# Larger row blocks in fewer buffers: five blocks of 32 and 56 rows per partition in place of eight of 32

## Chip, cores and metric

One core of a Trainium2 chip runs the kernel. The metric is the device time of one execution in microseconds (us); lower is better. All ratios below use runs in the fast state, against runs of the kernel before on the same chip in the same session; a slow run (over 1.5% above the fastest of the same kernel) is named and left out. Runs 1 to 4, 5 to 8 and 9 to 11 had one chip and session each, in which the kernel before took 163.67, 163.64 and 163.60 us, so times may be compared across them to some tenths of a us. A ratio is the mean time of one kernel's fast runs over the mean of the other's fast runs of the same rounds, so it is not quite the ratio of the medians that are quoted.

## The reference

```python
x: (16, 2048, 256) float32          # 32768 rows of 256
W_adapted    = W + scale * (lora_A @ lora_B)                  # 256 x 256
W_norm       = np.sqrt(np.sum(W_adapted ** 2, axis=0, keepdims=True) + 1e-8)
W_final      = W_adapted / W_norm * m
y            = x.reshape(-1, 256) @ W_final                   # float32 out
```

Computing `W_final` is small. The bulk is to read 33.6 MB of x, multiply by one 256 x 256 matrix, and write 33.6 MB of y.

## The kernel before

x is cut into blocks; a block gives every partition `DJ` = 32 consecutive rows of 1 KB, so its load has one 32 KB descriptor per partition (a descriptor is one contiguous piece of a transfer; the trace records each as one packet, 128 for a load). A transfer has *landed* when the last of the 16 DMA engines has reported its completion. The result overwrites x in the same SBUF buffer and is stored from there. There are five such buffers.

```python
DJ = 32; NBLK = 8; XBUFS = 5
...
parts = [(b * CH, CH) for b in range(NBLK - 1)]                # seven whole blocks
parts += [(NCH - CH, CH // 2), (NCH - CH // 2, CH // 2)]       # the last: two halves
...
for n in range(len(parts)):                  # SyncE: all loads
    b = parts[n][0] // CH
    if b >= XBUFS and parts[n][0] % CH == 0:
        nc.sync.wait_ge(sem(f"store{b - XBUFS}"), 16)          # buffer free?
    load_x(n)
```

The compute is a pipeline over 32 *pairs*, a pair being 8 rows per partition (two groups of `J` = 4 rows). GpSimd rounds a pair to bf16, TensorE transposes it, VectorE copies the transposes to SBUF, TensorE multiplies, ScalarE copies the two halves of the product back into the x buffer and issues the store when a stored part is complete. TensorE's loop handles two pairs per turn:

```python
turned(0)
with nc.Fori(0, NPR // 2, 1, engines=[PE], head_slot={PE: 128}):
    turned(1)      # transposes of pair 2i+1: waits until it is rounded
    product(0)     # product of pair 2i
    product(1)     # product of pair 2i+1
    turned(0)      # transposes of pair 2i+2
```

So the product of an even pair stands *behind* the transposes of the odd pair after it. With blocks of 32 rows (4 pairs), every block begins at an even pair, and the two never belong to different blocks.

## Time and profile before

| | before |
|---|---|
| time, median | 163.63 us (163.5 to 163.79) |
| span of the profiled execution | 163.2 us (this execution took 164.71) |
| busy share PE, ACT, POOL, DVE | 65%, 39%, 38%, 29% |
| bytes moved, mean rate | 67.41 MB, 413 GB/s |

From the page of the kernel before, the span in 40 equal slices of 4.08 us; a digit is the busy share in tenths, 9 meaning 90% or more:

```profile
## 2 busy tenths in 40 slices
PE   1270599789789897898981998619988820892000
DMA  5998998998999999999999999999999999998991
GB/s 201 402 498 386 426 474 385 482 418 265 466 426 426 442 410 466 426 394 482 418 426 442 420 426 458 402 458 410 446 414 454 414 446 422 450 442 377 442 430 60
```

The DMA row is at 8 or 9 from the second slice to the last but one, while TensorE has idle slices at the end. The 265 GB/s of the tenth slice is the one dip of the middle. The queue part of the same page (queue, packets, megabytes, share of 16 engines' span) says the same in sums:

```profile
q1 hardware_dynamic: 1440, 33.82, 49.0%
q10 hardware_dynamic: 1474, 33.59, 47.8%
```

q1 carries the loads, q10 the stores; together they fill 96.8%. The kernel is bound by its DMA engines. Waits of compute engines are therefore harmless as long as transfers stay queued. The waits of the kernel before (engine, line, what it waited for, total us, times, longest):

```profile
ACT x_sb L219 <- PE y_ps L281: 75.8, 33, 13.2
POOL xb L165 <- DMA x_sb<-in_x_dram: 56.0, 6, 12.2
```

GpSimd waits 56 us for loads, ScalarE 75.8 us for products, and neither costs anything here. The chain that ended last ascribes to them only the end:

```profile
## 4 chain that ended last, share of the span: by engine, by line
ACT 1%; PE 1%; issue 0%
```

Last, how long a block's compute takes once its load has landed. This is the second half of the last block, from the timeline of the kernel before (start, duration, engine, line, operation, and in brackets the idle time before it and what ended it; L165 rounds, L219 copies the product, L128 issues the store):

```profile
137.23 3.73 POOL L165 CAST xb<-x_sb 128x2048 bf16<-128x2048 f32 x2 [11.14 <-DMA x_sb<-in_x_dram]
143.94 1.93 ACT L219 COPY x_sb<-y_ps 128x1024 f32<-128x1024 f32 x2 [11.19 <-PE y_ps L281]
148.20 0.34 ACTq L128 DMA_DIRECT2D out_dram<-x_sb  x1
```

16 rows need 11.0 us from the first rounding to the issue of the store.

### The profile page before, as it was taken

To read this page: it belongs to the slowest core of one execution; us is meant where nothing else is said; L and a number is where in the kernel's file an instruction comes from. 1 tells how busy PE (TensorE), PEld (TensorE's weight loads), DVE (VectorE), ACT (ScalarE), POOL (GpSimd) and SP (SyncE) were. 2 spreads that over 40 slices of the span, in tenths; PEclk is the share of its full clock that TensorE was granted. 3 is DMA by queue.
4 is the path that set the end of the run, shared out by engine and by line. 5 is a ranking of instruction groups with operands and counts; after the bars stand their busy time and mean duration, and the time that the engine had idled before them with its cause. 6 is when DMAs were issued, how large, how long until landed. Compare 5 with 4: busy or idle time off the path is not lost. (4 is left out here: it accounts for less than half of the span.)

```text
span 163.2 us, 1988 instructions
## 1 busy us (share of the span) xinstructions
PE 105.3 (65%) x786; PEld 85.2 (52%) x786; DVE 47.2 (29%) x44; ACT 63.8 (39%) x67; POOL 62.5 (38%) x39
## 2 busy tenths in 40 slices
PE   1270599789789897898981998619988820892000
PEld 0130577677577775776760867418676610771000
DVE  0429452350532514405230325005051400330000
ACT  3010027548366384473754053900738440062000
POOL 1006381753935738268004940069209003900000
PEclk9999999999999999999998589985899996599755
DMA  5998998998999999999999999999999999998991
GB/s 201 402 498 386 426 474 385 482 418 265 466 426 426 442 410 466 426 394 482 418 426 442 420 426 458 402 458 410 446 414 454 414 446 422 450 442 377 442 430 60
DMA packets 2915, 67.41 MB, mean 413 GB/s; under 512 B 465, under 2 KB 482, under 8 KB 610
## 3 DMA queue, kind: packets, MB, share of 16 engines
q1 hardware_dynamic: 1440, 33.82, 49.0%
q10 hardware_dynamic: 1474, 33.59, 47.8%
q14 instruction: 1, 0.01, 0.0%
HBM read 33.85 MB, written 33.55 MB: 413 GB/s over the span
## 5 line engine op out<-in xcount | busy, mean ns | idle before, releaser
L219 ACT COPY x_sb<-y_ps 128x1024 f32<-128x1024 f32 x64 | 61.9, 1014 | 75.8 <-PE y_ps L281 75.8
L165 POOL CAST xb<-x_sb 128x2048 bf16<-128x2048 f32 x32 | 60.0, 1902 | 79.3 <-DMA x_sb<-in_x_dram 56.0
L281 PE MATMUL y_ps<-w_final,xt 128*128 128x256 bf16 x512 | 64.6, 280 | 12.8 <-PEq L256 12.8
L202 DVE COPY xt<-xt_ps 128x1024 f32<-128x1024 f32 x32 | 38.2, 1221 | 88.1 <-PE xt_ps L267 88.0
L281 PEld LDWEIGHTS y_ps<-w_final,xt 128*128 128x128 bf16 x512 | 48.4, 100 | 28.2 <-issue 19.8
L267 PE MATMUL xt_ps<-identity,xb 128*128 128x128 f32 x264 | 39.1, 309 | 23.1 <-PEq L256 23.1
L267 PEld LDWEIGHTS xt_ps<-identity,xb 128*128 128x128 f32 x264 | 34.9, 161 | 25.8 <-issue 25.6
L198 DVE TENSOR_TENSOR w_final<-wam,rnorm 128x256 bf16<-128x256 f32 x2 | 4.0, 2028 | 0.0
L244 PE MATMUL y_ps<-sq,ones 128*128 128x256 f32 x4 | 2.1, 674 | 1.6 <-DVE sq L187 1.6
L233 PE MATMUL y_ps<-identity,a_nat 128*16 128x128 f32 x2 | 0.6, 397 | 3.6 <-DMA a_nat<-in_lora_A_dram 3.6
L212 ACT ACTIVATE norm<-y_ps,eps_col 128x256 f32<-128x256 f32 x1 | 0.5, 473 | 6.1 <-PE y_ps L244 6.1
L244 PEld LDWEIGHTS y_ps<-sq,ones 128*128 128x128 f32 x4 | 1.2, 323 | 2.3 <-DVE sq L187 2.1
L210 ACT ACT_TABLE_LOAD x1 | 1.3, 1283 | 2.4 <-issue 2.4
L233 PEld LDWEIGHTS y_ps<-identity,a_nat 128*16 128x16 f32 x2 | 0.1, 90 | 3.6 <-issue 3.6
L171 POOL MEMSET xb<- 128x2048 bf16 x1 | 1.8, 1805 | 0.3 <-PE xt_ps L267 0.3
L195 DVE RECIPROCAL rnorm<-norm 128x256 f32<-128x256 f32 x1 | 1.7, 1745 | 0.0
L237 PE MATMUL y_ps<-b_bf,aT 16*128 16x256 bf16 x2 | 0.6, 404 | 1.5 <-DVE aT L180 1.5
L189 DVE COPY m_all<-y_ps 128x256 f32<-128x256 f32 x1 | 0.4, 425 | 3.3 <-PE y_ps L249 3.3
L178 DVE CAST b_bf<-b_nat 16x256 bf16<-16x256 f32 x1 | 0.3, 281 | 3.8 <-DMA b_nat<-in_lora_B_dram 3.8
L249 PE MATMUL y_ps<-m_row,ones 1*128 1x256 f32 x2 | 1.2, 710 | 0.0
L237 PEld LDWEIGHTS y_ps<-b_bf,aT 16*128 16x128 bf16 x2 | 0.1, 106 | 1.9 <-DVE aT L180 1.9
L183 DVE SCALAR_TENSOR_TENSOR wa<-y_ps,w_nat 128x512 f32<-128x512 f32 x1 | 0.7, 692 | 0.8 <-PE y_ps L237 0.8
(13 smaller groups left out, 3.7 us busy)
## 6 DMA issues: line engine op xcount, KB each, us to landing
x_sb<-in_x_dram SPq DMA_DIRECT2D x7, 4096.0 KB, 27.1
out_dram<-x_sb ACTq DMA_DIRECT2D x7, 4096.0 KB, 37.2
x_sb<-in_x_dram SPq DMA_DIRECT2D x2, 2048.0 KB, 29.6
out_dram<-x_sb ACTq DMA_DIRECT2D x2, 2048.0 KB, 20.2
w_nat<-in_W_dram SPq DMA_DIRECT2D x1, 256.0 KB, 2.9
a_nat<-in_lora_A_dram ACTq DMA_DIRECT2D x1, 16.0 KB, 2.6
b_nat<-in_lora_B_dram ACTq DMA_DIRECT2D x1, 16.0 KB, 3.6
m_row<-in_m_dram ACTq DMA_DIRECT2D x1, 1.0 KB
```

The costliest lines, as they stand in the source:

```text
L165: nc.gpsimd.tensor_copy(out=xb_bufs[p % NXB][:], in_=x_bufs[b % XBUFS][:, 2 * c * J : 2 * (c + 1) * J, :],).then_inc(sem("rounded"), 1)
L171: nc.gpsimd.memset(xb_bufs[NPR % NXB][:], 0.0).then_inc(sem("rounded"), 1)
L183: nc.vector.scalar_tensor_tensor(out=wa[:], in0=ab_ps, scalar=float(scale), in1=w_nat[:], op0=ALU.mult, op1=ALU.add).then_inc(dv, 1)
L195: nc.vector.reciprocal(out=rnorm[:], in_=norm[:]).then_inc(dv, 1)
L198: i = nc.vector.tensor_mul(out=w_final[:, t], in0=wam[:, t], in1=rnorm[:])
L202: nc.vector.tensor_copy(out=xt_bufs[p % NXT][:].rearrange("p r t -> p (r t)").bitcast(FP32), in_=xt_ps[p % 2][:],).then_inc(sem("copied"), 1)
L210: nc.scalar.activation(out=warm[:], in_=eps_col[:], func=AF.Sqrt)
L219: nc.scalar.copy(out=x_bufs[b % XBUFS][:, c * J : (c + 1) * J, :], in_=y_ps[g % 2][:]).then_inc(sem("room"), 1)
L244: i = nc.tensor.matmul(n2_ps, ones[:], sq[:, t, :], start=(t == 0), stop=(t == KC - 1))
L249: nc.tensor.matmul(mb_ps, ones[0:1, :], m_row[:], start=True, stop=True).then_inc(pe, 1)
L267: i = nc.tensor.transpose(xt_ps[p % 2][:, j * P : (j + 1) * P], xb_bufs[p % NXB][:, j, :].bitcast(FP32), identity[:],)
L281: i = nc.tensor.matmul(y_ps[h][:, j, :], xt_bufs[p % NXT][:, r : r + P, t], w_final[:, t, :], start=(t == 0 and (j % (J // 2)) == 0), stop ...
```

## The change

The intent: fewer and longer descriptors (up to 56 KB in place of 32 KB) save a fixed cost on each. 168 KB of buffers per partition take the place of 160 KB, hence three buffers of 56 rows. The diff, cut to its core:

```diff
-    DJ = 32
-    BLK = DJ * P
-    NBLK = N // BLK
-    XBUFS = 5
+    BLOCKS = [32, 56, 56, 56, 56]
+    STORES = [[32], [56], [56], [56], [24, 16, 16]]
+    DJ = max(BLOCKS)
+    XBUFS = 3
 ...
-    parts = [(b * CH, CH) for b in range(NBLK - 1)]
-    parts += [(NCH - CH, CH // 2), (NCH - CH // 2, CH // 2)]
 ...
+    def load_x(b):                      # one load for each block, the last too
         nc.sync.dma_start(
-            out=in_sbuf(*parts[n]), in_=in_dram(x_flat, *parts[n])
-        ).then_inc(sem(f"load{n}"), 16)
+            out=x_bufs[b % XBUFS][:, 0 : BLOCKS[b], :], in_=in_dram(x_flat, b)
+        ).then_inc(sem(f"load{b}"), 16)
 ...
+    for b in range(len(BLOCKS)):
+        if b >= XBUFS:
+            ...  wait for every store of block b - XBUFS
+        load_x(b)
 ...
-        if p == 0 or part_of[2 * p - 1] != part_of[2 * p]:
-            nc.gpsimd.wait_ge(sem(f"load{part_of[2 * p]}"), 16)
+        if r == 0:                      # r: first row of this pair in its block
+            nc.gpsimd.wait_ge(sem(f"load{b}"), 16)
```

TensorE's loop and all compute instructions stay. Blocks now begin at pairs 0, 4, 11, 18 and 25.

More of the change, by code (lines that the diff above doesn't have):

```diff
@@ L36 @@
     J = 4
-    DJ = 32
-    BLK = DJ * P
-    NBLK = N // BLK
-    assert IN == OUT and IN % P == 0 and OUT % P == 0 and N % BLK == 0
-    XBUFS = 5
-    CH = DJ // J
-    NCH = NBLK * CH
+    BLOCKS = [32, 56, 56, 56, 56]
+    STORES = [[32], [56], [56], [56], [24, 16, 16]]
+    DJ = max(BLOCKS)
+    assert IN == OUT and IN % P == 0 and OUT % P == 0 and N == P * sum(BLOCKS)
+    XBUFS = 3
+    ROWS = sum(BLOCKS)
+    NCH = ROWS // J
     NPR = NCH // 2
-    PRB = CH // 2
     NXB = 2
@@ L94, with place @@
     mb_ps = y_ps[1][:, 2, :]
-    late = [nc.alloc_semaphore(f"store{b}") for b in range(NBLK - XBUFS, NBLK + 1)]
-    sems = {f"store{NBLK - XBUFS + k}": s for k, s in enumerate(late)}
+    starts = [sum(BLOCKS[:b]) for b in range(len(BLOCKS))]
+    stores = []
+    for b, cuts in enumerate(STORES):
+        assert sum(cuts) == BLOCKS[b]
+        for k, cnt in enumerate(cuts):
+            stores.append((b, sum(cuts[:k]), cnt))
+    last_store = {b: n for n, (b, _, _) in enumerate(stores)}
+    store_at = {starts[b] + r0 + cnt: n for n, (b, r0, cnt) in enumerate(stores)}
+    def place(row):
+        b = max(k for k in range(len(BLOCKS)) if starts[k] <= row)
+        return b, row - starts[b]
+    first_late = last_store[len(BLOCKS) - XBUFS - 1] + 1
+    late = [nc.alloc_semaphore(f"store{n}") for n in range(first_late, len(stores))]
+    sems = {f"store{first_late + k}": s for k, s in enumerate(late)}
     def sem(name):
@@ L103, in sem, with in_dram @@
         return sems[name]
-    parts = [(b * CH, CH) for b in range(NBLK - 1)]
-    parts += [(NCH - CH, CH // 2), (NCH - CH // 2, CH // 2)]
-    part_of = {}
-    for n, (g0, cnt) in enumerate(parts):
-        for g in range(g0, g0 + cnt):
-            part_of[g] = n
-    def in_sbuf(g0, cnt):
-        b, c = divmod(g0, CH)
-        return x_bufs[b % XBUFS][:, c * J : (c + cnt) * J, :]
-    def in_dram(dram, g0, cnt):
-        return dram[g0 * J * P : (g0 + cnt) * J * P].rearrange("(p j) k -> p j k", p=P)
-    def load_x(n):
+    def in_dram(dram, b):
+        r0 = starts[b] * P
+        return dram[r0 : r0 + BLOCKS[b] * P].rearrange("(p j) k -> p j k", p=P)
+    def load_x(b):
         nc.sync.dma_start(
-            out=in_sbuf(*parts[n]), in_=in_dram(x_flat, *parts[n])
-        ).then_inc(sem(f"load{n}"), 16)
+            out=x_bufs[b % XBUFS][:, 0 : BLOCKS[b], :], in_=in_dram(x_flat, b)
+        ).then_inc(sem(f"load{b}"), 16)
     def store_y(n):
+        b, r0, cnt = stores[n]
         nc.scalar.dma_start(
-            out=in_dram(out_flat, *parts[n]), in_=in_sbuf(*parts[n])
+            out=in_dram(out_flat, b)[:, r0 : r0 + cnt, :],
+            in_=x_bufs[b % XBUFS][:, r0 : r0 + cnt, :],
         ).then_inc(sem(f"store{n}"), 16)
@@ L140 @@
     nc.scalar.dma_start(out=m_row[:], in_=m[None, :]).then_inc(sem("load_m"), 16)
-    for n in range(len(parts)):
-        b = parts[n][0] // CH
-        if b >= XBUFS and parts[n][0] % CH == 0:
-            nc.sync.wait_ge(sem(f"store{b - XBUFS}"), 16)
-        load_x(n)
+    for b in range(len(BLOCKS)):
+        if b >= XBUFS:
+            for n in range(len(stores)):
+                if stores[n][0] == b - XBUFS:
+                    nc.sync.wait_ge(sem(f"store{n}"), 16)
+        load_x(b)
     nc.gpsimd.memset(zeros[:], 0.0).then_inc(sem("pool"), 1)
@@ L159 @@
     for p in range(NPR):
-        b, c = divmod(p, PRB)
-        if p == 0 or part_of[2 * p - 1] != part_of[2 * p]:
-            nc.gpsimd.wait_ge(sem(f"load{part_of[2 * p]}"), 16)
+        b, r = place(2 * J * p)
+        if r == 0:
+            nc.gpsimd.wait_ge(sem(f"load{b}"), 16)
         if p >= NXB:
@@ L166 @@
             out=xb_bufs[p % NXB][:],
-            in_=x_bufs[b % XBUFS][:, 2 * c * J : 2 * (c + 1) * J, :],
+            in_=x_bufs[b % XBUFS][:, r : r + 2 * J, :],
         ).then_inc(sem("rounded"), 1)
@@ L215 @@
     for g in range(NCH):
-        b, c = divmod(g, CH)
+        b, r = place(J * g)
         nc.scalar.wait_ge(sem("product"), g + 1)
         nc.scalar.copy(
-            out=x_bufs[b % XBUFS][:, c * J : (c + 1) * J, :], in_=y_ps[g % 2][:]
+            out=x_bufs[b % XBUFS][:, r : r + J, :], in_=y_ps[g % 2][:]
         ).then_inc(sem("room"), 1)
-        n = part_of[g]
-        if g == NCH - 1 or part_of[g + 1] != n:
+        n = store_at.get(J * (g + 1))
+        if n is not None:
             nc.scalar.drain().then_inc(sem("done"), 1)
```

## The prediction

> **What bounds it now.** The DMA engines. The 40-slice table has DMA at 9 or more in nearly every slice up to the end; the queue table adds up to 96.8% of 16 engines' span; no compute engine is over 65%. The trace's packet records show one descriptor per partition: 32 KB in 1.213 us, 16 KB in 0.611 us, so about 0.009 us fixed each and 27 GB/s per engine. Per engine 156.4 us of packets lie between 1.97 us (first weight packet) and about 160.2 us; some 1.9 us are lost once, where load packets stretch to 2 to 2.9 us around the first store. One engine ends 2.5 us behind, at 163.2. With loads and stores both queued, packets alternate one for one (the Trainium skill, "DMA: Bandwidth & Descriptors", "Queues, rings and completion order", says packet-wise round robin; this trace agrees). The chain of waits blames only the last copies, 1%; the stores behind them are what ends last.
>
> **What the change removes.** Per engine 144 data packets become 96: 48 x 0.009 = 0.43 us. Five completion packets less: 0.05 us. Bytes and compute instructions stay. So at most 0.5 us (0.3%) is to be gained where there is no idle DMA.
>
> **What it adds: coarser dependences, on the critical path.** The load of block 3 waits for store 0, that of block 4 for store 1. Before, five buffers kept a load or a store always queued.
>
> 1. First gap. By store 0's landing the engines have done 24 load and 8 store packets: 53.3 us of work, ending near 58 us on most engines, 60 us on the slowest (before, store 0 landed at 58.1 to 60.6). Store 1 isn't issued by then, load 3 only now: first packet about 1 us after issue (first issues in the timeline: 0.9 to 1.9 us). So about 61.3 us; most engines idle some 2 to 3 us.
>
> 2. Second gap, the larger one. PE's loop works on pairs of 8 rows: transposes of pair 2i+1, products of 2i and 2i+1, transposes of 2i+2. Before, every block began at an even pair. Now blocks begin at pairs 4, 11, 18, 25. Pairs 11 and 25 are odd, so the product of the last pair of block 1 (block 3) stands behind transposes that need block 2 (block 4). Store 3 therefore can't be issued before load 4 has landed. After 61.3 us 16 load and 16 store packets of 2.116 us remain: loads and store 2 are done near 129 us. Then, from the timeline at 137 us of before: cast 1.9, transposes 1.8 (after idling), product 1.9 to 2.7, copy 1.0, drain and issue 0.2, first packet 1.0: about 8 us with DMA empty.
>
> 3. Tail. Stores 3 and 4 need 33.8 us more per engine: 137.5 + 33.8 = 171.3. The pieces of 24, 16, 16 rows (issued near 145, 152, 158 us by 6.6 us per 16 rows) are ready in time and hide nothing further.
>
> Timed runs lie 0.4 us above the span (163.63 against 163.2); up to 1 us of engine lag may remain. I predict 171.7 us, 8 in 10 between 168.8 and 174.5. Chances: faster 0.02, same 0.08, slower 0.90.
>
> **What would show it.** Right: DMA slices near 0 to 3 around 129 to 137 us, a smaller dip near 60; issue of store 3 about 7 us after load 4's landing, POOL waiting for that load just before; packets of 56 KB near 2.12 us. Wrong: store 3 issued before load 4 lands; DMA full throughout, then 163 us; the early 1.9 us stretch absent; 56 KB packets slower per byte.
>
> **What would make it wrong.** Loads running ahead of stores (early landing of load 4 shrinks gap 2), the slow engine's lag absorbed in the gaps, or packets cut smaller by the hardware.

## The result, and the profile after

The time is 176.63 us (176.18 to 176.73) against 163.69 us of the kernel before: a ratio of 1.0787 (95% interval 1.0765 to 1.0808). The change is slower, as predicted, but by 12.9 us where 8.0 had been forecast (171.7 less 163.7), and outside the stated range of 168.8 to 174.5.

The 40 slices of the kernel after, now of 4.36 us each:

```profile
## 2 busy tenths in 40 slices
PE   1533988398976797897308978910006978986000
DMA  5999999977998699999999999999940499979997
GB/s 195 473 413 565 434 421 421 421 331 331 451 541 361 210 421 368 434 434 421 434 423 421 421 434 421 421 421 421 447 184 0 210 421 421 421 329 423 417 421 304
```

There is a hole in the DMA row at slices 30 to 32 (126 to 140 us), with one slice at 0 GB/s, and a smaller dip at the 14th slice (57 to 61 us, 210 GB/s). The queues:

```profile
q1 hardware_dynamic: 864, 33.82, 46.6%
q10 hardware_dynamic: 1186, 33.59, 44.8%
```

The packets are fewer as intended, and the engines were busy for 91.4% of a longer span. This is the hole, from the timeline of the kernel after (L171 rounds, L273 transposes, L287 is the product, L225 its copy, L132 the store):

```profile
130.35 3.73 POOL L171 CAST xb<-x_sb 128x2048 bf16<-128x2048 f32 x2 [20.95 <-DMA x_sb<-in_x_dram]
132.39 1.94 PE L273 MATMUL xt_ps<-identity,xb 128*128 128x128 f32 x8 [18.34 <-PEq L262]
134.12 5.18 PE L287 MATMUL y_ps<-w_final,xt 128*128 128x256 bf16 x32
136.07 2.06 ACT L225 COPY x_sb<-y_ps 128x1024 f32<-128x1024 f32 x2 [21.84 <-PE y_ps L287]
138.24 0.34 ACTq L132 DMA_DIRECT2D out_dram<-x_sb  x1
```

GpSimd waited 20.95 us for load 4 and rounded pair 25. TensorE had waited 18.34 us; only after transposing pair 25 did it multiply pair 24, the last of block 3. ScalarE had been idle 21.84 us. So the store of block 3 (56 rows, 7.3 MB) went out at 138.24 us, 7.9 us after load 4's landing. From 130.0 us, when the last packet of load 4 ended, to 139.1 us no data packet was moved. The waits with their new totals:

```profile
ACT x_sb L225 <- PE y_ps L287: 88.9, 32, 21.8
POOL xb L171 <- DMA x_sb<-in_x_dram: 61.8, 5, 20.9
```

And the first dip, two lines of the same timeline: load 3 is issued when store 0 has landed, store 1 five microseconds later.

```profile
58.08 0.33 SPq L126 DMA_DIRECT2D x_sb<-in_x_dram  x1
63.42 0.37 ACTq L132 DMA_DIRECT2D out_dram<-x_sb  x1
```

The trace also records each packet. Summed by hand over the 16 engines ("stretched" is the time of packets above the usual 1.213 us for 32 KB, 0.611 us for 16 KB and 2.116 us for 56 KB; all are us per engine):

```
                                                before    after
idle, middle: first gap near 58 us                0.0       1.65
idle, middle: gap 128.6 to 139.2 us               0.0      10.07
idle, end: some engines done before the slowest   3.15      1.08
stretched packets, all                            1.65      3.4
fixed cost of descriptors saved                      -      0.5
```

Idle time grew by 9.7 us and stretching by 1.8 us, less 0.5 us saved: 11.0 us, against 174.5 - 163.2 = 11.3 us between the spans. So the profile says where the time went. It does not say what would bring it back. For that I ran eleven kernels; all gave correct results.

### The profile page after: what moved, and what is told of

Same layout as the page of the kernel before. It is cut to its first block, busy times and chain, and to the rows that moved or that the text cites. A ratio compares the mean times of both kernels' runs of the same rounds, so it can differ in the third digit from the quotient of the medians.

```text
span 174.5 us, 1975 instructions
## 1 busy us (share of the span) xinstructions
PE 104.2 (60%) x786; PEld 84.4 (48%) x786; DVE 44.0 (25%) x44; ACT 63.7 (37%) x67; POOL 62.4 (36%) x39
## 5 line engine op out<-in xcount | busy, mean ns | idle before, releaser
L225 ACT COPY x_sb<-y_ps 128x1024 f32<-128x1024 f32 x64 | 61.8, 1014 | 88.9 <-PE y_ps L287 88.9
L171 POOL CAST xb<-x_sb 128x2048 bf16<-128x2048 f32 x32 | 59.9, 1896 | 89.0 <-DMA x_sb<-in_x_dram 61.8
L287 PE MATMUL y_ps<-w_final,xt 128*128 128x256 bf16 x512 | 64.7, 279 | 12.6 <-PEq L262 12.4
L287 PEld LDWEIGHTS y_ps<-w_final,xt 128*128 128x128 bf16 x512 | 48.6, 100 | 27.8 <-issue 19.4
L273 PE MATMUL xt_ps<-identity,xb 128*128 128x128 f32 x264 | 38.2, 303 | 37.5 <-PEq L262 37.5
L273 PEld LDWEIGHTS xt_ps<-identity,xb 128*128 128x128 f32 x264 | 34.0, 158 | 40.0 <-issue 39.8
L255 PEld LDWEIGHTS y_ps<-m_row,ones 1*128 1x128 f32 x2 | 0.5, 308 | 0.7 <-issue 0.7
L204 DVE TENSOR_TENSOR w_final<-wam,rnorm 128x256 bf16<-128x256 f32 x2 | 0.8, 421 | 0.0
```

The source lines that it names most:

```text
L171: nc.gpsimd.tensor_copy(out=xb_bufs[p % NXB][:], in_=x_bufs[b % XBUFS][:, r : r + 2 * J, :],).then_inc(sem("rounded"), 1)
L204: i = nc.vector.tensor_mul(out=w_final[:, t], in0=wam[:, t], in1=rnorm[:])
L225: nc.scalar.copy(out=x_bufs[b % XBUFS][:, r : r + J, :], in_=y_ps[g % 2][:]).then_inc(sem("room"), 1)
L255: nc.tensor.matmul(mb_ps, ones[0:1, :], m_row[:], start=True, stop=True).then_inc(pe, 1)
L273: i = nc.tensor.transpose(xt_ps[p % 2][:, j * P : (j + 1) * P], xb_bufs[p % NXB][:, j, :].bitcast(FP32), identity[:],)
L287: i = nc.tensor.matmul(y_ps[h][:, j, :], xt_bufs[p % NXT][:, r : r + P, t], w_final[:, t, :], start=(t == 0 and (j % (J // 2)) == 0), stop ...
```

## The experiments

Theory at the start ("parity"): the hole is made by TensorE's order, since blocks 2 and 4 begin at odd pairs, 11 and 25. Rivals: three coarse buffers starve the DMA whatever the order, or packets of 56 KB are slow.

### 1. The order on TensorE alone

```diff
-    with nc.Fori(0, NPR // 2, ...):  turned(1); product(0); product(1); turned(0)
+    with nc.Fori(0, 5, ...):         turned(1); product(0); product(1); turned(0)
+    product(0); turned(1); product(1); turned(0)      # pair 10 before pair 11
+    with nc.Fori(0, 6, ...):         turned(1); product(0); product(1); turned(0)
+    product(0); turned(1); product(1); turned(0)      # pair 24 before pair 25
+    with nc.Fori(0, 3, ...):         turned(1); product(0); product(1); turned(0)
```

> The changed kernel with PE's loop cut so that the products of pairs 10 and 24 come before the transposes of pairs 11 and 25; same blocks, buffers and descriptors. Parity theory: store 1 (was issued at 63.4 us) goes out near 59 us, store 3 (was 138.2 us, after load 4's landing at 130.3) goes out before load 4 lands, the 10 us of empty DMA shrink below 2 us, time 165 to 168 us (ratio to before 1.01 to 1.03). Rival, three coarse buffers starve the DMA whatever the order on PE: store 3 still waits, gap stays over 6 us, time 173 us or more.

Measured: 172.24 us (median of three fast runs, 171.6 to 173.11; one slow run of 182.22), ratio 1.0524 (1.0459 to 1.0589). The stores did what the theory said: store 1 went out at 59.3 us and store 3 at 124.9 us, before load 4 landed. But only 4.4 of the 12.9 us came back, and a hole is there again, some 15 us later. Slices of this run (4.26 us each):

```profile
DMA  5999999999979599999999999999999999049978
```

The timelines of this run tell why. GpSimd begins to round block 4:

```profile
133.30 3.74 POOL L171 CAST xb<-x_sb 128x2048 bf16<-128x2048 f32 x2 [17.76 <-DMA x_sb<-in_x_dram]
```

and ScalarE copies products and issues the four last stores:

```profile
124.86 0.34 ACTq L132 DMA_DIRECT2D out_dram<-x_sb  x1
140.74 1.01 ACT L225 COPY x_sb<-y_ps 128x1024 f32<-128x1024 f32 x1 [15.99 <-PE y_ps L287]
...
151.01 0.34 ACTq L132 DMA_DIRECT2D out_dram<-x_sb  x1
...
157.62 0.34 ACTq L132 DMA_DIRECT2D out_dram<-x_sb  x1
...
164.22 0.34 ACTq L132 DMA_DIRECT2D out_dram<-x_sb  x1
```

Block 4 was rounded from 133.30 us on, and its 56 rows took until 164.22 us, 30.9 us. Store 3, no longer held, was finished at 146 us on most engines, and the first piece of block 4 came only at 151.01 us. The packet records show 5.4 us idle per engine between. The cause that the prediction named is real, but with it gone the time is limited by the compute on the last block, whose single load lands too late. Parity theory: its mechanism stands, its claim to the time falls.

### 2. Even starts with three buffers

```diff
-    BLOCKS = [32, 56, 56, 56, 56]
-    STORES = [[32], [56], [56], [56], [24, 16, 16]]
+    BLOCKS = [32, 32, 48, 48, 48, 48]
+    STORES = [[32], [32], [48], [48], [48], [16, 16, 16]]
```

> Blocks of 32, 32, 48, 48, 48, 48 in three buffers of 48 rows, last block stored as 16, 16, 16: every block starts at an even pair, PE's loop untouched. Parity theory: no store is held by a later load, no DMA gap over 2 us, time 162 to 166 us (ratio 0.99 to 1.015). Rival, three buffers or descriptors over 32 KB cost by themselves: 168 us or more.

Measured: 165.35 us, ratio 1.0093 (1.0065 to 1.0121), with a gap of 1.4 us near 48 us and of 1.1 us near 158 us. So three buffers and 48 KB descriptors cost about 1% when the sizes suit; neither forces a loss of 8%. This run changes sizes and parity together and cannot tell them apart. One thing in it bears on what follows: its last load is uncut as well (48 rows, landed at 132.2 us), and yet the only gap after it is the one of 1.1 us. The store of block 4, held by nothing, was issued at 128.8 us and ran to 147.6 us, and the first piece of the last block, of only 16 rows, was issued at 144.4 us, in time.

### 3. Three buffers in the kernel before

```diff
-    XBUFS = 5
+    XBUFS = 3
```

> The kernel before with three buffers of 32 rows in place of five, nothing else. Lookahead alone, with even starts. Theory: some small gaps, loads land later and the last block's compute shows at the end, 166 to 169 us (ratio 1.015 to 1.035). Rival, the buffer count explains the whole loss of the change: 174 us or more.

Measured: 171.63 us, ratio 1.0503 (1.0455 to 1.0551), between the two expectations and outside both. The slices of this run (4.25 us each) show where:

```profile
DMA  5989898559599898989899999599999999999996
```

Loads 0 to 2 are done at 32.6 us, but the first store's packets start only at 36.0 us (3.4 us idle); a gap of 1.8 us follows at 46 us and one of 1.6 us at 107 us. Load packets are stretched there too (2.9 us per engine over all loads, against 1.5 before). Lookahead (how many loads may be issued before a store has to free a buffer) is worth 5% to this kernel, with even starts and 32 KB descriptors.

### 4. Odd starts with five buffers

```diff
-    BLOCKS = [32, 56, 56, 56, 56];  XBUFS = 3
+    BLOCKS = [24, 32, 32, 32, 32, 32, 32, 24, 16];  XBUFS = 5     # each stored whole
```

> Blocks of 24, six of 32, 24, 16 in five buffers of 32 rows, so seven blocks start at an odd pair, with the lookahead of before. Theory: an odd start only costs where no other transfer is queued, so the held stores hide behind queued ones: within 1% of before (162 to 165 us). Rival, an odd start costs about the same 5 to 10 us wherever it is: 170 us or more.

Measured: 163.48 us, ratio 0.9983 (0.9955 to 1.0011), the same as before, no gap of note before the end. Seven of nine blocks begin at an odd pair. With five buffers, where other transfers were queued, odd starts cost nothing.

### 5. The last load cut again

Experiment 1 pointed at a part of the change that I had overlooked: the last block's load is no longer cut. Everything else stays as in the change, the odd starts too.

```diff
+    LOADS = [[32], [56], [56], [56], [24, 32]]       # one semaphore for each piece
```

> The changed kernel with only the load of its last block cut again, in pieces of 24 and 32 rows with a semaphore each (the kernel before had two loads of 16 rows there, the change made it one of 56). PE's order stays as in the change, so pair 24's product still waits for pair 25, but pair 25 now needs only the first piece, which should land near 113 us instead of 130. New theory, the loss is what the uncut last load holds back (store 3 through the odd pair, then 31 us of compute on 56 rows): store 3 issued before 122 us, no DMA gap over 2 us after 60 us, time 164 to 167 us. Rival, the odd pair or the three buffers cost by themselves: 171 us or more.

Measured: 167.71 us (167.2 to 168.2), ratio 1.0238 (1.0199 to 1.0276). One cut in one load brings back 8.9 of the 12.9 us. The time is just above the 164 to 167 expected, and one step was misjudged: the first piece was rounded from 121.2 us, not near 113, so that store 3 left at 128.66 us and not before 122. Timelines of this run: GpSimd,

```profile
121.19 3.73 POOL L175 CAST xb<-x_sb 128x2048 bf16<-128x2048 f32 x2 [12.09 <-DMA x_sb<-in_x_dram]
130.88 3.73 POOL L175 CAST xb<-x_sb 128x2048 bf16<-128x2048 f32 x2 [3.75 <-DMA x_sb<-in_x_dram]
```

and ScalarE:

```profile
128.66 0.34 ACTq L136 DMA_DIRECT2D out_dram<-x_sb  x1
137.50 0.34 ACTq L136 DMA_DIRECT2D out_dram<-x_sb  x1
```

The first piece released pair 25, and with it pair 24 and store 3, at 128.66 us, just as the loads were running out (their last packets end at 129.1 us on most engines). And the 24 rows of the first stored piece were ready at 137.50 us, long before store 3 was through at 146.6 us. The one edit takes away both what experiment 1 removed and what it ran into. In the 40 slices the hole is gone; the dip of the 14th to 17th slice stays:

```profile
DMA  5999999998989699699999998998998999989993
```

### 6. Both mends

The edits of 1 and 5 together.

> Both mends, the reordered products of the first run and the cut last load. New theory: the reorder adds nothing once the load is cut, so within 1% of the kernel with only the cut load, 164 to 167 us. Rival, the two costs are separate and add up: the reorder gains its 4 us again, to 160 to 163 us.

Measured: 167.46 us (median of three fast runs, 167.25 to 167.58; one slow run of 175.89), ratio 1.0224 (1.0189 to 1.026). The reorder adds nothing once the load is cut. The two costs do not add: they stand one behind the other on the way from the last load to the last stores.

### 7. Half descriptors

```diff
+    # each load and each store in two halves, one semaphore, waits of 32 for 16
+    h = BLOCKS[b] // 2
+    for r0 in (0, h): nc.sync.dma_start(... r0 : r0 + h ...).then_inc(sem(f"load{b}"), 16)
```

> The changed kernel with every load and store issued as two halves (descriptors of 8 to 28 KB), both counted on one semaphore, so every wait and block is as in the change. Theory, descriptor size is not the cause, only the dependences are: gap near 129 us stays at 8 to 11 us, time 174 to 178 us, and the stretch of load packets and the delay to a first store packet (6.0 us for store 1) get shorter since fewer bytes stand ahead. Rival, packets of 56 KB are the loss: 168 us or less.

Measured: 176.28 us, ratio 1.0756 (1.0719 to 1.0793). With descriptors of at most 28 KB and the same waits, the loss is whole, the gap 10.7 us (129.0 to 139.9). The slices of this run (4.38 us each):

```profile
DMA  5999999999999799999999999999930299999997
```

So the size of the packets is not the cause. The delay from the issue of store 1 to its first packet fell from 6.0 to 4.9 us, the stretch from 3.4 to about 3.1 us per engine: a small effect.

### 8. Four buffers of 40 rows

```diff
+    BLOCKS = [32, 32, 32, 40, 40, 40, 40];  XBUFS = 4      # last loaded and stored as 24, 16
```

> A try at a version better than both: blocks of 32, 32, 32, 40, 40, 40, 40 in four buffers of 40 rows, last block loaded and stored as 24 and 16. Descriptors up to 40 KB, four blocks of lookahead. Theory: no gap over 1 us, 161.5 to 164.5 us, that is within 1% of before; the 0.3 us of saved descriptor cost will hardly show. Rival, odd starts (pairs 17 and 27) cost with four buffers: 167 us or more.

Measured: 163.65 us, ratio 1.0006 (0.9975 to 1.0038): no loss, no visible gain from the longer descriptors.

### 9. Filling the first gap

4 us were left after experiment 5. Block 0 has 32 of the 56 rows of its buffer, so rows 32 to 55 of block 3 may be loaded there without waiting for store 0. This is no lifted wait but a place that nobody uses.

```diff
-    LOADS = [[32], [56], [56], [56], [24, 32]]
+    LOADS = [[32], [56], [56], [32, 24], [24, 32]]
+    ... after load 2: load rows 32-55 of block 3; then wait for store 0, load rows 0-31
```

> The kernel with the cut last load, and the load of block 3 cut in rows 0 to 31 and rows 32 to 55 too; the latter lie where block 0 never was (it has 32 rows of the 56 in that buffer), so they are loaded right after block 2 without a wait. Theory: the remaining 4 us over before are the first gap (1.8 us near 58 us, loads waiting for store 0) and load packets stretched by about 1.5 us more than before; this fills the gap, and the 16 stretched packets at the restart of the loads near 59 us go with it (0.7 us): 164.5 to 166.5 us, no gap over 0.5 us before 120 us. Rival, three buffers cost in some other way: no change, 167 us or more.

Measured: two fast runs, 165.07 and 165.46 us, and two slow ones (168.13, 170.24), against a median of 163.60 before; with two fast runs there is no interval. The first gap is gone, and so are the stretched packets near 59 and 66 us: the stretch of load packets sums to 1.6 us per engine, nearly all of it in load 2, in place of 3.0 in run 5.

### 10. Block 1 stored in two pieces as well

```diff
-    STORES = [[32], [56], [56], [56], [24, 16, 16]]
+    STORES = [[32], [24, 32], [56], [56], [24, 16, 16]]
```

> The same with block 1 also stored in pieces of 24 and 32 rows, so that the first piece goes out near 48 us, while store 0 is still in flight, and the store queue never runs empty until the end. Theory, load packets stretch where a store is issued into an empty store queue beside loads: the second stretch (packets of 3.1 to 4.0 us at 66 to 70 us, about 1.3 us per engine) goes, and 163.5 to 165.5 us is left. Rival, stretching comes with 56 KB load packets beside any store: the summed stretch stays above 2.5 us per engine, time as the run before.

Measured: 163.99 us (163.55 to 164.63), ratio 1.0024 (0.999 to 1.0059). The slices of this run (4.07 us each) are nearly full again; the 6 in the 31st is a gap of 1.1 us near 126 us:

```profile
DMA  5999999979898899999899979899996999999993
```

With the edits of runs 5, 9 and 10 together all of the loss is recovered, with three buffers, odd starts and most of the 56 KB descriptors (loads 1 and 2, the stores of blocks 2 and 3) still there. What this run's own edit adds is not shown. Load packets stretched by 0.9 us per engine, against 1.6 in run 9, but the difference lies in load 2 between 34 and 39 us, before the first piece of block 1 was issued at 45.2 us, and run 9 had two fast runs only. The theory of stretching in the expectation is not supported, though. In run 9 the store queue was empty from 60.2 to 67.7 us, store 1 started beside loads, and those load packets (24 and 32 KB there) were not stretched. What stretches packets stays open.

### 11. The uncut load in the kernel before

```diff
+    BLOCKS = [32] * 8;  STORES = [[32]] * 7 + [[16, 16]];  XBUFS = 5     # loads whole
```

> The kernel before (eight blocks of 32, five buffers) with only its last block's load left uncut, its store still in two pieces of 16. Theory: an uncut last load costs only what it holds back beyond the stores already queued; here the stores of blocks 5 and 6 are queued and run to about 150 us, so it is free: within 0.6% of before, 163 to 164.6 us. Rival, an uncut last load costs by itself: 168 us or more.

Measured: 163.94 us, ratio 1.0015 (0.9994 to 1.0036). Here an uncut last load was free: stores queued before it covered what it holds back.

## Why the prediction was wrong

The direction, the place of the loss and its mechanism were right. The steps that failed are three terms of the sum, each too small: the gap with DMA empty, the tail, and the step from span to time (items 3 to 5). As an account of the cause the prediction was also incomplete (item 6).

1. *What bounds it.* Right. DMA-bound before, and longer descriptors gained at most 0.5 us (runs 7 and 8 show nothing more).
2. *First gap.* Right in place and kind: load 3 issued at 58.08 us when store 0 had landed. It was 1.65 us, where "some 2 to 3 us" was predicted. The loads and stores up to there were expected to be done "near 129 us" and ended at 128.6 to 130.0 us. That was luck, since two errors cancelled: loads restarted at 59.0 us and not at 61.3, and load 3 then lost 2.1 us per engine to stretched packets, at 59 and at 66 us, which it had not counted.
3. *Second gap.* The mechanism was there instruction by instruction. "About 8 us with DMA empty" was mis-sized: 10.07 us. The prediction counted from the load's end on a typical engine, 128.9 us, but rounding waits for the slowest of 16 engines and started at 130.35 us; and the step from rounding to the store's issue took 7.9 us, where its terms sum to 6.8 to 7.6 us. The first packet of store 3 began at 139.1 us, not 137.5: 1.6 us.
4. *Tail.* "33.8 us more" was mis-sized: the last packet ended at 174.0 us on the slowest engine, 34.9 us after the restart, and the landing was recorded 0.5 us later, for which no term stood: 1.6 us.
5. *From span to time.* "Timed runs lie 0.4 us above the span" compared a median with the span of another execution. The profiled execution of before itself took 164.71 us with a span of 163.2 us, 1.5 us more; after, it is 176.18 against 174.5, 1.7 us. This mis-sized term is 1.3 us.

Items 3 to 5 add up to 4.5 us, and 171.7 + 4.5 = 176.2 us is the time of the profiled execution (the median is 0.4 us more). So the miss is three terms of the sum, none of them large.

6. *What the prediction did not see.* "The pieces of 24, 16, 16 rows ... are ready in time" held in the changed kernel: the first was issued at 147.07 us, and store 3 ran to 156.2 us. So this is no part of the miss. But the pieces were in time only because the gap had delayed store 3, and the order on TensorE, which the prediction gives as the cause of the larger gap, is only part of that cause. When the order was mended (run 1), the pieces came too late, and only 4.4 of 12.9 us came back. I had read the diff as changing block sizes, buffers and parity, and missed that it also dropped the cut in the last load. Restoring that one cut, odd starts and all, gave 8.9 us (run 5), and the reorder on top of it nothing (run 6).

What the runs support in its place: near the end the DMA engines had no work because 56 rows arrived in one landing, and everything that could be stored afterwards stood behind it, first store 3 through the odd pair, then the first piece of block 4. The other 4 us are mostly the first gap and the stretch that came with it: run 9 (two fast runs, so without an interval) removes about 2.4 us, and runs 9 and 10 together remove all of it. Runs 4 and 11 show that neither an odd start nor an uncut last load costs anything by itself with five buffers, and run 2 that an uncut last load can cost little with three, where no store is held and the first stored piece is small; run 7 shows that packet size is not it; run 3 shows that too little lookahead alone can cost 5%.

On the Trainium skill: its page "DMA: Bandwidth & Descriptors", section "Queues, rings and completion order", says that each engine serves its queues in turn, packet by packet. The trace agrees: with both queues filled, load and store packets alternate one for one (a completion of 4 bytes takes a turn as well). The page calls 9 to 17 descriptors typical for a packet; here each packet record is one descriptor, of 16 to 56 KB. The section "Issuing engines are not separate DMA queues" of that page says that transfers from different issuers share the same 16 engines. The trace agrees: by the packet records of the kernel before, the load queue alone moves 432 GB/s (14 to 32 us), and both together move 433 (68 to 85 us).

No run beat the kernel before beyond the noise; the best, run 4, is 0.2% faster with an interval that includes 1.

## What to carry to other kernels

In a kernel bound by DMA, look for what is queued at every moment, and cost a change by the longest stretch in which nothing is: a coarser last load holds back every store that depends on it, so cut the last load as well as the last store. When a profile shows a wait that ends a gap, ask what the time would be limited by if that wait were gone; here the named wait was real, and removing it uncovered another one some 15 us later. A dependence across blocks, such as a loop that handles two items per turn, cost nothing visible here where other transfers were queued (runs 4, 8 and 10); where it held the last store that could have been queued, in the changed kernel, the DMA engines were empty for 10 us.

## What the Trainium skill lacked or had wrong

- "DMA: Bandwidth & Descriptors", "Bandwidth" advises transfers of 1 MiB or more; no page gives the time of one descriptor of tens of KB. Here 32 KB took 1.213 us and 56 KB 2.116 us, 27.0 and 27.1 GB/s per engine: beyond 32 KB there is hardly anything left to gain.
- The same page, "Latency and other measured facts", gives about 0.6 us to the first byte for transfers issued from SyncE or ScalarE. With idle engines I measured 0.8 to 1.0 us from issue to first packet, but 6.0 us when loads of 56 KB packets were under way (store 1 of the kernel after). The page has no figure for a busy queue.
- The same page, "Anatomy of one DMA", puts most of about 2 us of fixed cost (for transfers issued from GpSimd) into the write receipt. Here, issued from SyncE, a load's completion came 0.3 to 0.5 us after the last packet of each engine with nothing else queued (load 4 of the kernel after), but 2.5 to 2.6 us after it with 56 KB store packets queued beside it (load 4 of run 1). In that trace the completion packets start 2.1 us after the last data packets, which is the length of one 56 KB store packet: the completion stands behind a store packet in the turn-taking. The page has no figure for that.
- No page has the stretched packets: 32 KB load packets of up to 2.9 us and 56 KB ones of up to 4.0 us (in run 2 also 32 KB store packets of up to 2.3 us), in a window of up to some 6 us around the start of a store or the restart of loads, 0.3 to 1.7 us lost per engine each time, and sometimes none. Their cause is open.
